# A mixture-of-experts stage that fetches its tokens row by row by indirect transfers in place of one-hot products

## The chip, the cores and the metric

One core of a Trainium2 chip runs the whole program. The metric is device time in microseconds (us), the median of several runs; smaller is better. The engines of the core are named as in the profile: PE (TensorE), DVE (VectorE), ACT (ScalarE), POOL (GpSimd), SP (SyncE, which here only issues transfers).

## The reference

Two layers of a hybrid network on 512 tokens of width 1024, all in fp32. Each layer mixes tokens (sparse attention, a gated delta rule, a convolution, an out-projection), normalizes, sends the tokens through a mixture of experts, and normalizes again. The change lies in the mixture of experts:

```python
g_w, g_idx = lax.top_k(softmax(xt @ w_group + b_group), 1)         # 1 of 4 groups
e_val, e_loc = lax.top_k(e_in, 2)                                  # 2 of its 8 experts
e_w = softmax(e_val) * g_w
...
hid = silu(xb @ w_gate[e]) * (xb @ w_up[e])                        # xb: the expert's tokens
y = hid @ w_down[e]                                                # 1024 -> 512 -> 1024
...
out[token] += y * e_w                                              # back to the token's row
```

There are 32 experts a layer, each with 6 MB of weights (gate, up, down), and 512 tokens times 2 experts = 1024 pairs.

## The kernel before, in words

**The MoE stage.** The router counts the tokens of each expert and sorts the experts by count. The sorted expert of rank r gets a fixed number of slots, `CAPS[r]` (L33): 192, 128, 96, 64 or 32. Nine *cycles* (`CYCLES`, L34) take the ranks in an order written out by hand; a cycle's experts fill up to 256 slots, in one or two *units* of 128. Cycle 0 holds two experts that are fixed beforehand (ranks 30 and 31, 64 slots each), so that work can begin before the sort is done; the other cycles hold two to five experts. There are 17 units a layer. Weights don't stay on the chip: each expert's come as six tiles of 1 MB, four of gate/up (`w_gu`, L1174, two transfers of 512 KB each) and two of down (`w_d`, L1179), all issued on SP in the order of the cycles, into a ring of 3 + 8 = 11 tiles (`ering`, L1162). A tile's transfer can start when the matmuls that read the tile's last content are done.

**What a cycle needs before its experts can run.** `prep_oh` (DVE, L1331 and L1339) compares the tokens' positions with a row of counts and so builds the one-hot matrix `m_oh` (512 tokens x up to 256 slots). `gather` multiplies it on PE with the normalized tokens (L1363). The tokens are kept as two rounded parts, `x1h` and `x1l` (split on ACT, POOL and DVE at L1193 and L1194 while the router works), so that fp32 values pass through the fast fp32r matmuls: 64 matmuls of 256 columns a cycle, in four pieces `kp`. `affine` (L1347 on ACT, L1349 on DVE) scales the result into `m_xe`, with the tokens' features on the partitions. `prep_ws` multiplies the one-hot with the router's weights (L1373) and picks each slot's weight (`m_wsl`, DVE L1380). `prep_T` transposes the one-hot on PE (L1388) and copies it (`m_ohT`, L232 on ACT or L234 on DVE) for the scatter.

**An expert.** `ffn` (L1251): gate/up matmuls `f_gu` (L1263 for 128 slots, L1267 for fewer), silu and weight on ACT and DVE (L1273, L1274), transposes `f_hT` (L1282) and their copy (L1284), down matmuls `f_y` (L1299). `y_split` (L1307, L1309) cuts the result into two fp32r parts, and `scatter` adds it to the tokens' rows: four matmuls `m_sc` with `m_ohT` (L1398) and an add on DVE (L1399) for each of 4 blocks of tokens.

**What sets the order.** PE runs this stage in program order. Inside `ffn`, while ACT and DVE make `f_h` and while `f_hTs` is copied, `fill` takes pieces from a queue (gather, prep_ws, prep_T, scatter) and so puts PE work there; the pieces of a cycle are spread over its experts, two places for each. The other engines are ordered by a scheduler that follows the program. A branch behind the nine cycles (L1468), for experts with more tokens than slots, isn't taken with these inputs. `residual` (behind the first expert) scales the tokens on POOL and loads the second normalization's weights on ACT's queue (L237).

## Time and profile before

| | us |
|---|---|
| median of 3 runs | 2047.71 (2028.74, 2047.71, 2047.86) |
| profiled execution, its own time | 2042.02 |
| its span, first to last instruction | 2040.3 |
| MoE stage of layer 0, first `f_gu` to last `f_y` | 448.5 to 995.5 |
| MoE stage of layer 1 | 1463.1 to 2009.4 |

The span is shorter than the time by 1.7 us, which lie around it. The mean granted PE clock of the profiled execution is 0.940 of 2.4 GHz. A timeline row gives start and length of a group of like instructions; lengths of neighbouring PE rows overlap, since matmuls are pipelined, so what a group costs on PE is read from the distance of the starts. Idle time stands in brackets with the event that ended it.

### The profile page before, as it was taken

How to read it: one execution, taken by the hardware profiler on the slowest of the kernel's cores; microseconds unless marked ns; L12 is line 12 of the kernel's file. 1: busy time of each engine (PE TensorE's matmuls, PEld its weight loads, DVE VectorE, ACT ScalarE, POOL GpSimd, SP SyncE). 2: the span in 40 equal slices, each digit the busy share in tenths (PEclk: the TensorE clock that was granted, in tenths of full speed). 3: DMA queues.
4: the chain of work that ended last, by engine and by line, in shares of the span. 5: the costliest groups of instructions: out<-in, count | busy, mean ns of one | idle time of the engine just before them, and what ended most of it. 6: DMA issues, size and time to landing. Idle time of an engine off the chain costs nothing. (4 is left out here: it accounts for less than half of the span.)

```text
span 2040.3 us, 33443 instructions
## 1 busy us (share of the span) xinstructions
PE 1858.5 (91%) x12956; PEld 1158.7 (57%) x12956; DVE 1028.8 (50%) x2148; ACT 600.3 (29%) x1275; POOL 363.3 (18%) x320
## 2 busy tenths in 40 slices
PE   8898799879999999998789988999699999999996
PEld 6776676654555545433378766767445555444433
DVE  2766866564332344323637777765543423443245
ACT  3333655432111111111233336453211111111122
POOL 2335632313000000000122356223130000000001
PEclk9997799989999999999989877989899999999998
DMA  5231001729999979888722310016299999798985
GB/s 174 90 96 63 1 12 35 272 81 351 403 408 386 357 281 408 311 304 325 272 94 83 104 42 1 23 61 252 88 354 404 408 372 350 293 408 311 334 318 193
DMA packets 141458, 465.41 MB, mean 228 GB/s; under 512 B 20345, under 2 KB 22897, under 8 KB 141297
## 3 DMA queue, kind: packets, MB, share of 16 engines
q1 hardware_dynamic: 137152, 452.54, 59.0%
q10 hardware_dynamic: 4144, 10.70, 1.5%
q8 instruction: 104, 1.70, 0.3%
q14 instruction: 58, 0.47, 0.1%
HBM read 459.00 MB, written 4.19 MB: 227 GB/s over the span
## 5 line engine op out<-in xcount | busy, mean ns | idle before, releaser
L1267 PE MATMUL f_gu<-w_gu,m_xe 128*32 128x256 f32 (+1 forms) x3456 | 391.9, 451 | 12.7 <-ACT m_xe L1347 6.2
L1267 PEld LDWEIGHTS f_gu<-w_gu,m_xe 128*32 128x32 f32 (+1 forms) x3456 | 134.0, 118 | 260.5 <-issue 200.4
L1299 PE MATMUL f_y<-w_d,f_hTs 128*32 128x256 f32 (+2 forms) x1824 | 250.1, 472 | 8.0 <-DVE m_wsl L1380 4.6
L1309 DVE TENSOR_TENSOR m_yl<-f_y,m_yh 32x256 fp32r<-32x256 f32 (+2 forms) x222 | 115.4, 520 | 260.6 <-ACT m_yh L1307 231.9
L1307 ACT CAST m_yh<-f_y 32x256 fp32r<-32x256 f32 (+2 forms) x222 | 98.3, 443 | 302.5 <-PE f_y L1299 300.3
L1274 DVE SCALAR_TENSOR_TENSOR f_h<-f_h,m_wsl,f_gu 128x128 f32<-128x128 f32 (+1 forms) x76 | 33.1, 435 | 292.3 <-ACT f_h L1273 291.8
L1299 PEld LDWEIGHTS f_y<-w_d,f_hTs 128*32 128x32 f32 (+2 forms) x1824 | 81.7, 123 | 152.6 <-issue 130.5
L1399 DVE TENSOR_TENSOR xr<-xr,m_sc 128x1024 f32<-128x1024 f32 x128 | 151.7, 1218 | 20.5 <-PE m_sc L1398 19.9
L1363 PE MATMUL m_g<-m_oh,x1h 128*128 128x256 f32 x576 | 146.7, 294 | 0.4 <-DVE m_oh L1339 0.3
L1363 PE MATMUL m_g<-m_oh,x1l 128*128 128x256 f32 x576 | 142.1, 286 | 0.0
L1273 ACT ACTIVATE f_h<-f_gu 128x128 f32<-128x128 f32 (+1 forms) x76 | 26.4, 347 | 350.0 <-PE f_gu L1267 258.0
L1398 PE MATMUL m_sc<-m_yh,m_ohT 128*128 128x512 f32 (+1 forms) x256 | 114.1, 446 | 14.8 <-DVE xr L1399 7.6
L1363 PEld LDWEIGHTS m_g<-m_oh,x1h 128*128 128x128 f32 x576 | 111.3, 193 | 15.6 <-issue 12.2
L344 POOL TENSOR_TENSOR w_hl<-w_slice,w_hl 128x512 fp32r<-128x512 f32 (+1 forms) x54 | 70.3, 1303 | 238.7 <-ACT w_hl L343 229.6
L216 POOL TENSOR_TENSOR ln_rs<-ln_rs,mhalf 128x1 f32<-128x1 f32 x16 | 8.6, 548 | 580.1 <-DVE ln_rs L293 580.1
L1363 PEld LDWEIGHTS m_g<-m_oh,x1l 128*128 128x128 f32 x576 | 111.5, 194 | 0.1
L1398 PE MATMUL m_sc<-m_yl,m_ohT 128*128 128x512 f32 (+1 forms) x256 | 102.1, 399 | 0.0
L343 ACT CAST w_hl<-w_slice 128x512 fp32r<-128x512 f32 (+1 forms) x96 | 56.0, 589 | 130.4 <-PE ipB L350 120.4
L879 POOL MEMSET vcb<- 128x512 f32 x2 | 1.0, 524 | 501.9 <-PE f_y L1299 501.7
L1263 PE MATMUL f_gu<-w_gu,m_xe 128*128 128x512 f32 x192 | 87.7, 603 | 0.0
L759 POOL TENSOR_TENSOR cvt<-cvt,cv_t 128x485 f32<-128x485 f32 (+28 forms) x66 | 78.3, 1187 | 13.8 <-ACT cv_t L755 12.0
L1398 PEld LDWEIGHTS m_sc<-m_yh,m_ohT 128*128 128x128 f32 (+1 forms) x256 | 48.8, 191 | 55.9 <-DVE xr L1399 22.2
(468 smaller groups left out, 3578.5 us busy)
## 6 DMA issues: line engine op xcount, KB each, us to landing
w_gu<-in_moe_w_gate SPq DMA_DIRECT2D x256, 512.0 KB, 10.9
w_gu<-in_moe_w_up SPq DMA_DIRECT2D x256, 512.0 KB, 10.4
w_d<-in_moe_w_down SPq DMA_DIRECT2D x128, 1024.0 KB, 11.4
w_slice<-in_w_in SPq DMA_DIRECT2D x20, 1024.0 KB, 5.2
w_out<-in_w_out SPq DMA_DIRECT2D x16, 1024.0 KB, 8.3
...
```

What stands on the lines that cost most here:

```text
L343: A.copy(hi[:, :n], src)
L344: (G if LOE(npc[0], k) else V).tensor_tensor(lo[:, :n], src, hi[:, :n].bitcast(F32), op=ALU.subtract)
L759: G.tensor_tensor(ac2[:, 30 - j:512], ac2[:, 30 - j:512], tm, op=ALU.add)
L1263: T.matmul(pg[:, i, :], xe(k), wv[:, i, :], start=(k == 0), stop=(k == 7), skip_group_check=True)
L1267: T.matmul(pg[j * c:(j + 1) * c, 0, 0:2 * fw], xe(k), wv[:, :, j * fw:(j + 1) * fw], start=(k == 0), stop=(k == 7), skip_group_check=True)
L1274: V.scalar_tensor_tensor(hh[:, :fw], hh[:, :fw], ws(), gu[:, fw:2 * fw], op0=ALU.mult, op1=ALU.mult)
L1299: T.matmul(o, lt, wv[:, n * nw:(n + 1) * nw], start=(k == 0), stop=(k == 3), skip_group_check=True)
L1307: A.copy(hi[:, n * nw:(n + 1) * nw], src[n])
L1309: V.tensor_tensor(lo[:, n * nw:(n + 1) * nw], src[n], hi[:, n * nw:(n + 1) * nw].bitcast(F32), op=ALU.subtract)
L1363: T.matmul(ps[:, kk * 256:kk * 256 + 256], src[t][:, k * P:(k + 1) * P], OH[cy][:, t, :], start=(t == 0 and i == 0), stop=(t == NT - 1 and ...
L1398: T.matmul(ps2[:, n, :], ohT[0:nr, t * P:(t + 1) * P], y[0:nr, n * 512:(n + 1) * 512], start=(i == 0), stop=(i == 1))
L1399: V.tensor_tensor(xr[t][:, :D], xr[t][:, :D], ps2.rearrange("p a b -> p (a b)"), op=ALU.add)
```

## The change

The one-hot products with the tokens are gone, and with them `x1h` and `x1l`. The normalized tokens are written to DRAM, block by block, on SP's queue (`x1D`). For each cycle a new step `index` multiplies the one-hot (now bf16) with a small matrix: each token's number in two bf16 parts, and the sorted weights in three bf16 parts, 98 columns in all. One such product of four matmuls a unit gives, for each slot, the token's number and the weights. DVE adds the parts, POOL issues an indirect transfer per unit (`tokens`), which fetches 128 rows of 4 KB from `x1D` into a tile `XG`; a slot without a token has a number above 511, and its row isn't fetched. `gather` is now eight PE transposes a unit out of `XG`, 16 a cycle. `prep_T` is one comparison on DVE of each slot's token number with a row of counts (`m_iot`), without PE. `index` of the next cycle goes to the front of the queue of `fill` when a cycle starts, and its gather stands in the queue behind the scatters that are left over. Cycle 0's tokens are fetched ahead of the loop, and its weights and `index(1)` come inside its first expert. The freed memory makes the ring 3 + 9 + 1 = 13 tiles. Lines after the change are shifted by 7 to 43.

The core of the diff:

```diff
-CN=32, XL="GGGV", ..., R=3, R2=8, NG=10, NE=15
+CN=32, ..., R=3, R2=9, R4=1, NG=10, NE=9
...
                 A.activation(xr[t][:, :D], xr[t][:, :D], AF.Identity, scale=rs, bias=nb)
+                nc.sync.dma_start(x1D[l][t * P:(t + 1) * P, :], xr[t][:, :D])
...
-            i = en[0] % (R + R2)
+            i = en[0] % (R + R2 + R4)
...
-            A.copy(av, xv)
-            (V if XL[t] == "V" else G).tensor_tensor(bv, xv, av.bitcast(F32), op=ALU.subtract)
...
+        XG = [x4(f"xg{i}") for i in range(2)]
+        for xg in XG:
+            G.memset(xg[:, :D], 0.0)
...
+        tw = small("r_tw", [P, NT, 98], BF16, bufs=1)
+        V.tensor_copy(tw[:, :, 0:2], tokb)
+        parts3(tw[:, :, 2:98], srt[:, :, 1, :], 32)
...
-            if width(cy) < 256:
-                V.tensor_scalar(ohv[:, :, width(cy):], ...)
...
+        def tokens(cy, ps, k):
+            tok, idx = small("m_tok", [P, 2]), small("m_idx", [P, 2], I32)
...
+                V.tensor_reduce(tok[0:n, u], v[0:n, u, 0:2], axis=AX.X, op=ALU.add)
+                V.tensor_scalar(idx[0:n, u], tok[0:n, u], float(PAD), None, op0=ALU.add)
+            for u in units(cy):
+                n = rows(cy, u)
+                G.indirect_dma_start(XG[u][0:n, :D], None, x1D[l][:, :], bass.IndirectOffsetOnAxis(ap=idx[0:n, u:u + 1], axis=0),
+                                     bounds_check=S - 1, oob_is_err=False)
...
+        def place_mm(cy, ps, k, rhs):
+            for u in units(cy):
+                for t in range(NT):
+                    T.matmul(ps[0:n, u * k:(u + 1) * k], OH[cy][:, t, u * P:u * P + n], rhs[:, t, :], ...)
...
+        def index(cy):
+            ps = bank("m_ix")
+            place_mm(cy, ps, 98, tw)
+            tokens(cy, ps, 98)
+            slot_weights(cy, ps, 98, 2, 32)
...
         def gather(cy, kp):
...
-                for t in range(NT):
-                    for i, src in enumerate((x1h, x1l)):
-                        T.matmul(ps[:, kk * 256:kk * 256 + 256], src[t][:, k * P:(k + 1) * P], OH[cy][:, t, :], ...)
+                for u in units(cy):
+                    m = rows(cy, u)
+                    T.transpose(ps[:, kk * 256 + u * P:kk * 256 + u * P + m], XG[u][0:m, k:1024:8], ident[0:m, 0:m])
...
         def prep_T(cy, u):
-            for t in range(NT):
-                T.transpose(ps[0:n, t * P:(t + 1) * P], OH[cy][:, t, u * P:u * P + n].bitcast(F32), ident)
-            evac(ohT[0:n], ps[0:n])
+            V.tensor_scalar(ohT[0:n], iot[0:n], TOK[cy][0:n, u:u + 1], None, op0=ALU.is_equal)
...
             if cy + 1 < len(JOBS):
                 prep_oh(cy + 1)
-                queue.extend([(gather, cy + 1, kp) for kp in range(4)] + [(prep_ws, cy + 1)])
+                if cy:
+                    queue.appendleft((index, cy + 1))
+                queue.extend((gather, cy + 1, kp) for kp in range(4))
```

**Where instructions move.** The start of layer 0's MoE stage on PE, before: the first gather is cut in two by the sort (`r_swp`, `r_sorted`, `r_ids`, `r_cnt`), and the first gate/up matmuls `f_gu` follow it.

```order
L1221 MATMUL r_swp<-ident,r_sw_3516 64x128 x2
L1363 MATMUL m_g_4189<-m_oh,x1h_4096 128x256
L1363 MATMUL m_g_4189<-m_oh,x1l_4097 128x256
...
L1226 MATMUL r_sorted<-r_pm,r_swT 128x64 x4
L1230 MATMUL r_ids<-r_pm,cst 1x32
L1238 MATMUL r_cnt<-r_pm,r_cntd 128x32
...
L1363 MATMUL m_g_4189<-m_oh,x1l_4109 128x256
L1267 MATMUL f_gu<-w_gu,m_xe_4187 64x512 x4
L1373 MATMUL m_ws<-r_sw_3516,m_oh 128x32 x4
```

After, the sort comes first; the product that places cycle 0's tokens (`m_ix`), four transposes out of the fetched rows (`xg`) and the first gate/up matmuls follow.

```order
L1223 MATMUL r_swp<-ident,r_sw_3520 64x128 x4
L1228 MATMUL r_sorted<-r_pm,r_swT 128x64 x4
L1245 MATMUL r_ids<-r_pm,cst 1x32
L1253 MATMUL r_cnt<-r_pm,r_cntd 128x32
L1382 LDWEIGHTS m_oh
L1382 MATMUL m_ix_4202<-tokb,m_oh 128x2
...
L1382 MATMUL m_ix_4202<-tokb,m_oh 128x2
L1417 MATMUL m_g_4214<-ident,xg_4107 128x128 x2
L1417 MATMUL m_g_4232<-ident,xg_4107 128x128 x2
L1282 MATMUL f_gu<-w_gu,m_xe_4200 64x512 x2
```

Between `m_ix` and `m_g` PE now waits for DVE's sums, POOL's transfer and its landing; 32 matmuls went out and 4 transposes came in.

In cycle 4 (ranks 20 and 0; `f_gu` of 32 slots is rank 20's), before: the fill places hold scatters (`m_sc`) of cycle 3 and the gather of cycle 5.

```order
L1267 MATMUL f_gu<-w_gu,m_xe_5509 32x256 x16
L1267 MATMUL f_gu<-w_gu,m_xe_5510 32x256 x16
L1398 MATMUL m_sc<-m_yh,m_ohT 128x512
L1398 MATMUL m_sc<-m_yl,m_ohT 128x512
...
L1398 MATMUL m_sc<-m_yl,m_ohT 128x512
L1282 MATMUL f_hT<-ident,f_h 128x128
L1398 MATMUL m_sc<-m_yh,m_ohT 128x512
...
L1398 MATMUL m_sc<-m_yl,m_ohT 128x512
L1363 MATMUL m_g<-m_oh,x1h_4096 128x256
L1363 MATMUL m_g<-m_oh,x1l_4097 128x256
```

After, `index(5)` stands ahead of the same scatters, and the transposes that need its rows behind them.

```order
L1282 MATMUL f_gu<-w_gu,m_xe_5351 32x256 x16
L1382 LDWEIGHTS m_oh
L1382 MATMUL m_ix<-r_tw,m_oh 128x98
...
L1382 MATMUL m_ix<-r_tw,m_oh 96x98
L1434 MATMUL m_sc<-m_yh,m_ohT 128x512
L1434 MATMUL m_sc<-m_yl,m_ohT 128x512
...
L1434 MATMUL m_sc<-m_yl,m_ohT 128x512
L1417 MATMUL m_g<-ident,xg_4107 128x128
L1417 MATMUL m_g<-ident,xg_4108 128x96
L1417 MATMUL m_g<-ident,xg_4107 128x128
```

Sixteen scatter matmuls and one `f_hT` lie between the last `m_ix` of cycle 5 and the first transpose of its rows.

DVE in the routing of layer 0, before: among the steps that pick the second expert (`r_em`, `r_m`, `r_s`, `r_mv`, `r_oh`) stand the last split of the tokens (`x1l`) and the clearing of the one-hot's unused columns (L1331).

```order
L1076 SCALAR_TENSOR_TENSOR r_em<-r_oh_4017,r_em 128x64
L1059 TENSOR_REDUCE r_m_4014<-r_em 128x2
L1061 SCALAR_TENSOR_TENSOR r_s_4016<-r_em,r_m_4014,cst 128x32 x2
L1194 TENSOR_TENSOR x1l_4109<-xr_3796,x1h_4108 128x1024
L1331 TENSOR_SCALAR m_oh<-cst 128x4x128
L1063 TENSOR_REDUCE r_mv<-r_s_4016 128x2
L1082 TENSOR_TENSOR r_m_4014<-r_m_4014,r_m_4013 128x2
L1064 TENSOR_TENSOR r_oh_4018<-r_s_4016,r_mv 128x64
```

After, the same steps follow each other directly.

```order
L1083 SCALAR_TENSOR_TENSOR r_em<-r_oh_4025,r_em 128x64
L1066 TENSOR_REDUCE r_m_4022<-r_em 128x2
L1068 SCALAR_TENSOR_TENSOR r_s_4024<-r_em,r_m_4022,cst 128x32 x2
L1070 TENSOR_REDUCE r_mv<-r_s_4024 128x2
L1089 TENSOR_TENSOR r_m_4022<-r_m_4022,r_m_4021 128x2
L1071 TENSOR_TENSOR r_oh_4026<-r_s_4024,r_mv 128x64
```

The two instructions between `r_s` and `r_mv` are gone here, and POOL no longer splits the tokens beside them.

## Rows read from the trace of the kernel before

**Rows 1.** The profile page: busy time of the engines (busy us, share of the span, instructions), and the span in 40 equal slices (GB/s moved by the DMA engines).

```profile
PE 1858.5 (91%) x12956; PEld 1158.7 (57%) x12956; DVE 1028.8 (50%) x2148; ACT 600.3 (29%) x1275; POOL 363.3 (18%) x320
...
GB/s 174 90 96 63 1 12 35 272 81 351 403 408 386 357 281 408 311 304 325 272 94 83 104 42 1 23 61 252 88 354 404 408 372 350 293 408 311 334 318 193
```

**Rows 2.** Windows of the span: the end of the routing in layer 0, the MoE stage of layer 0 (first gate/up matmul to last down matmul) and that of layer 1. Columns: window, its length, busy us of PE, PE weight loads, DVE, ACT and POOL with counts, granted clock, DMA share, GB/s.

```profile
426.60:432.40 5.80, 0.00 (x0) 0.00 (x0) 5.80 (x5) 3.84 (x2) 5.64 (x2) 0.50 0.00 0
...
448.50:995.50 547.00, 524.76 (x3789) 263.54 (x3787) 207.77 (x413) 99.38 (x231) 19.40 (x8) 0.98 0.92 352
...
1463.10:2009.40 546.30, 523.94 (x3788) 262.06 (x3787) 209.22 (x414) 99.11 (x230) 19.36 (x8) 0.99 0.92 351
```

**Rows 3.** What PE waited for in the MoE stage of layer 0, 448 to 995 us: total us, times, longest.

```profile
PE m_sc L1398 <- DVE m_ohT L234: 4.2, 4, 3.3
...
PE f_y L1299 <- DVE m_wsl L1380: 2.3, 1, 2.3
...
PE m_ohp L1388 <- DVE m_wsl L1380: 2.1, 2, 1.4
...
PE f_gu L1267 <- DMA w_gu<-in_moe_w_up: 1.0, 1, 1.0
```

**Rows 4.** What SP's DMA queue waited for in the same stage (total us, times, longest).

```profile
SPq L1174 <- PE f_y L1299: 94.9, 21, 15.1
SPq L1174 <- DMA w_d<-in_moe_w_down: 67.2, 35, 3.0
```

**Rows 5.** Windows of 40 us inside the MoE stage of layer 0, columns as in rows 2.

```profile
600.00:640.00 40.00, 39.09 (x157) 17.87 (x150) 15.74 (x22) 4.55 (x10) 0.00 (x0) 1.00 1.03 409
...
720.00:760.00 40.00, 39.57 (x230) 16.70 (x231) 17.47 (x27) 6.09 (x13) 0.00 (x0) 1.00 0.80 294
```

**Rows 6.** PE's timeline in layer 0 around the first expert's end and the gather of cycle 1. Columns: start us, length us, engine, line, operation, out<-in, tile shapes, count, and in brackets idle time before it with its releaser. The cut rows between 471.41 and 477.25 are 47 further gather matmuls, alternately from x1l and x1h; those between 477.25 and 479.72 are 16 more.

```profile
460.06 0.44 PE L1282 MATMUL f_hT<-ident,f_h 128*128 128x128 f32 x2 [1.00 <-DVE f_h L1274]
460.96 3.65 PE L1299 MATMUL f_y<-w_d,f_hTs 128*64 128x512 f32 x16 [0.46 <-ACT f_hTs L1284]
464.45 7.04 PE L1267 MATMUL f_gu<-w_gu,m_xe 128*64 128x512 f32 x32
471.41 0.39 PE L1363 MATMUL m_g<-m_oh,x1h 128*128 128x256 f32 x1
...
477.25 0.38 PE L1282 MATMUL f_hT<-ident,f_h 128*128 128x128 f32 x2
...
479.72 1.87 PE L1373 MATMUL m_ws<-r_srt,m_oh 128*128 128x32 f32 x16
481.42 0.63 PE L1388 MATMUL m_ohp<-ident,m_oh 128*128 128x128 f32 x4
481.98 3.65 PE L1299 MATMUL f_y<-w_d,f_hTs 128*64 128x512 f32 x16
```

**Rows 7.** PE's instructions in the MoE stage of layer 0, 448.5 to 995.5 us, grouped by line and form: count, busy us, mean ns of one, idle before.

```profile
L1363 PE MATMUL m_g<-m_oh,x1h 128*128 128x256 f32 x265 | 66.1, 290 | 0.1
L1363 PE MATMUL m_g<-m_oh,x1l 128*128 128x256 f32 x265 | 64.1, 282 | 0.0
```

**Rows 8.** Windows as in rows 2, of the scatter's matmuls (L1398) alone in the MoE stage of layer 0.

```profile
448.50:995.50 547.00, 74.69 (x256) 45.63 (x256) 0.98 0.92 352
```

**Rows 9.** PE's timeline where the out-projection's result is transposed with the column stride 8 that the change uses too (L1141).

```profile
389.87 1.16 PE L1141 MATMUL x1T_ps<-ident,xr 128*128 128x128 f32 x8 [2.20 <-DVE xr L1134]
390.79 0.48 PE L348 MATMUL opA<-wo_hi,mh 128*128 128x512 f32 x1
```

**Rows 10.** PE's timeline in the routing of layer 0 and at the start of its MoE stage; the rows left out are the first gather's, the sorting's and the counting's.

```profile
436.77 0.19 PE L1202 MATMUL r_pos<-r_selb,trib 128*128 128x32 bf16 x1 [13.13 <-DVE r_selb L1078]
...
436.91 0.27 PE L1204 MATMUL r_pos<-r_selb,oneb 128*128 128x32 bf16 x4
437.11 0.37 PE L1206 MATMUL r_pos<-oneb,r_selb 128*64 128x1 bf16 x4
...
448.56 0.65 PE L1267 MATMUL f_gu<-w_gu,m_xe 128*64 128x512 f32 x2
```

**Rows 11.** DVE's timeline in the routing of layer 0.

```profile
426.67 5.62 DVE L1061 SCALAR_TENSOR_TENSOR r_s<-r_em,r_m,cst 128x32 f32<-128x32 f32 x2
...
433.36 0.41 DVE L1061 SCALAR_TENSOR_TENSOR r_s<-r_em,r_m,cst 128x32 f32<-128x32 f32 x2
433.69 1.99 DVE L1194 TENSOR_TENSOR x1l<-xr,x1h 128x1024 fp32r<-128x1024 f32 x1
```

**Rows 12.** POOL's timeline in the same stretch.

```profile
426.58 5.66 POOL L1194 TENSOR_TENSOR x1l<-xr,x1h 128x1024 fp32r<-128x1024 f32 x2 [4.14 <-issue]
```

**Rows 13.** ACT and its DMA queue (ACTq) while the experts' weights stream: two 512 KB loads, and the instructions that wait for them.

```profile
464.67 0.33 ACTq L237 DMA_DIRECT2D ln_w<-in_ln_w  x1
465.04 0.87 ACTq L237 DMA_DIRECT2D ln_b<-in_ln_b  x1
...
473.33 1.06 ACT L1411 ACTIVATE ln_w<-ln_w 128x1024 f32<-128x1024 f32 x1 [7.49 <-DMA ln_w<-in_ln_w]
...
476.13 1.06 ACT L1412 ACTIVATE ln_b<-ln_b 128x1024 f32<-128x1024 f32 x1 [1.34 <-DMA ln_b<-in_ln_b]
```

**Rows 14.** SP's DMA queue: the first load that the MoE stage of layer 0 issues, and the last one.

```profile
450.54 0.39 SPq L1179 DMA_DIRECT2D w_d<-in_moe_w_down  x1
...
979.78 1.95 SPq L1179 DMA_DIRECT2D w_d<-in_moe_w_down  x2
```

More of the change, by code (lines that the diff above doesn't have):

```diff
@@ L173, in hybrid_kernel @@
     x_res = dr.tile([S, D], F32, name="x_res")
+    x1D = [dr.tile([S, D], F32, name=f"x1D{l}") for l in range(layers)]
     ident = cp.tile([P, P], F32, name="ident")
@@ L1349, in affine, with slot_weights @@
                 V.tensor_scalar(out_, in_, w1c[:, k:k + 1], b1c[:, k:k + 1], op0=ALU.mult, op1=ALU.add)
+        def tokens(cy, ps, k):
+            tok, idx = small("m_tok", [P, 2]), small("m_idx", [P, 2], I32)
+            v = ps[:, 0:2 * k].rearrange("p (u k) -> p u k", k=k)
+            full = all(rows(cy, u) == P for u in units(cy)) and len(units(cy)) == 2
+            for n, u in ([(P, slice(0, 2))] if full else [(rows(cy, u), slice(u, u + 1)) for u in units(cy)]):
+                V.tensor_reduce(tok[0:n, u], v[0:n, u, 0:2], axis=AX.X, op=ALU.add)
[4 more added lines that the diff above has]
+                                     bounds_check=S - 1, oob_is_err=False)
+            TOK[cy] = tok
+        def place_mm(cy, ps, k, rhs):
+            for u in units(cy):
+                n = rows(cy, u)
+                for t in range(NT):
+                    T.matmul(ps[0:n, u * k:(u + 1) * k], OH[cy][:, t, u * P:u * P + n], rhs[:, t, :], start=(t == 0),
+                             stop=(t == NT - 1), skip_group_check=True)
+        def slot_weights(cy, ps, k, o, m):
+            sums = small("m_wsum", [P, 2, 32])
+            for u in units(cy):
+                n = rows(cy, u)
+                V.tensor_reduce(sums[0:n, u, 0:m], ps[0:n, u * k + o:u * k + o + 3 * m].rearrange("p (a m) -> p m a", a=3),
+                                axis=AX.X, op=ALU.add)
+            w = small("m_wsl", [P, 8])
+            for i, (r, b, c, o_) in enumerate(JOBS[cy]):
+                s_, r = o_ % P, r if cy else r - 30
+                for j in range(P // c):
+                    V.tensor_copy(w[j * c:(j + 1) * c, i:i + 1], sums[s_:s_ + c, o_ // P, r:r + 1])
+            WS[cy] = w
+        def index(cy):
[3 more added lines that the diff above has]
+            slot_weights(cy, ps, 98, 2, 32)
         def gather(cy, kp):
@@ L1402, in hybrid_kernel @@
         prep_oh(0)
+        ps0 = bank("m_ix0")
+        place_mm(0, ps0, 2, tokb)
+        tokens(0, ps0, 2)
         for kp in range(GI):
@@ L1499, in hybrid_kernel @@
-                ox = t4("o_x")
-                psx = bank2("o_g")
-                for hh in range(2):
+                ow = small("o_w3", [P, NT, 3], BF16, bufs=1)
+                parts3(ow, wc.unsqueeze(2), 1)
+                pso = bank("o_ix")
+                for o, n, rhs in ((0, 2, tokb), (2, 3, ow)):
                     for t in range(NT):
-                        for i, src in enumerate((x1h, x1l)):
-                            T.matmul(psx[:, hh, :], oh[:, t * P:(t + 1) * P], src[t][:, hh * 512:(hh + 1) * 512],
-                                     start=(t == 0 and i == 0), stop=(t == NT - 1 and i == 1))
@@ L1506, in hybrid_kernel @@
-                A.copy(ox[:, 0:512], psx[:, 0, :])
-                V.tensor_copy(ox[:, 512:1024], psx[:, 1, :])
-                pso = bank2("o_ohp")
-                for t in range(NT):
-                    T.transpose(pso[:, 0, t * P:(t + 1) * P], oh[:, t * P:(t + 1) * P].bitcast(F32), ident)
-                for t in range(NT):
-                    T.matmul(pso[:, 1, 0:1], oh[:, t * P:(t + 1) * P].bitcast(F32), wc[:, t:t + 1], start=(t == 0),
-                             stop=(t == NT - 1))
@@ L1514, in hybrid_kernel @@
-                V.tensor_copy(oT, pso[:, 0, :])
-                ws = small("o_wsl", [P, 1], bufs=1)
-                V.tensor_copy(ws, pso[:, 1, 0:1])
+                        T.matmul(pso[:, o:o + n], oh[:, t * P:(t + 1) * P], rhs[:, t, :], start=(t == 0), stop=(t == NT - 1),
+                                 skip_group_check=True)
+                ot, oi = small("o_tok", [P, 1], bufs=1), small("o_idx", [P, 1], I32, bufs=1)
+                V.tensor_reduce(ot, pso[:, 0:2], axis=AX.X, op=ALU.add)
@@ L1567, in hybrid_kernel @@
         moe.close()
+        ring3.close()
         ring2.close()
```

78 lines of the change are left out of this document (40 added, 38 removed).

## The prediction

> **What bounds the kernel now.** The page comes first: PE is busy for 91% of the span, DVE for half [rows 1]. A share over the whole span hides stages, so the next view is the same line's GB/s: two plateaus of some eleven slices at 272 to 408, where the experts' weights stream [rows 1]. Windows around them give two MoE stages of 547.0 and 546.3 us, 1093 of 2040, with PE busy for 524.8 us of the first [rows 2]. In that stage PE waits only 1.0 us for weights and a few us for small DVE results [rows 3]; its own instruction stream sets the pace. SP's queue in turn waits mostly for PE: 94.9 us for down matmuls that still hold a ring tile, against 67.2 us for transfers of its own [rows 4]. In 40-us windows the stream alternates between 409 GB/s, which it does not exceed, and 294, where the ring holds it [rows 5]. So PE bounds the stage, with the stream close behind: 32 experts of 6 tiles of 1.0486 MB are 201.3 MB, 493 us at 408 GB/s. What PE loses is worth its full size only until the stream is the later one.
>
> **What goes from PE, per layer.** In the stage 265 + 265 gather matmuls run [rows 7]. From 471.41 to 477.25 there are 48, 0.122 us each [rows 6]: 530 x 0.122 = 64.5 us. The products for the weights take 1.70 us per 16 (479.72 to 481.42) and there are 136: 14.5. The one-hots' transposes take 0.56 us per 4 (481.42 to 481.98), 17 units: 9.5 [rows 6]. Together 88.5 us, all on the engine that sets the pace. Of the waits of DVE's copies behind those steps (4.2 + 2.3 + 2.1 us [rows 3]) I take 6 to go.
>
> **What comes to PE.** 17 units x 8 transposes, 4 of them ahead of the stage: 132. The transposes with the same stride take 0.92 us from start to next start for 8, with a length of 1.16 [rows 9]: 0.115 to 0.145 us each, 15 to 19 us; I take 16.5. The placement has 68 matmuls of bf16 with 98 columns. The trace has none like them: four bf16 matmuls of 32 columns lie within 0.20 us [rows 10], 0.05 each, and a gather matmul of 256 columns took 0.122; 3.4 to 8.3 us, and 6.8 (0.10 each), nearer to the wider one, since weight loads of 128 rows come with each. The fill places get emptier. Where nothing fills them, the first expert shows 1.00 us before `f_hT` and 0.46 before `f_y` [rows 6]; eight gathers now put 0.5 us per piece there, not 2, and some places are covered by scatters, so I take 5 us a layer, between 0 (all covered) and 10.
>
> **The new wait.** A gather's rows come through a chain: DVE's two small instructions (about 0.5 us, plus what stands ahead of them, 1.5 in all), two issues on POOL, and the landing. No transfer issued by POOL runs beside the weight stream before. The nearest rows are two loads of 512 KB on ACT's queue beside it: issued at 464.67 and 465.04, their waiters start at 473.33 and 476.13 [rows 13], so 8.7 and 11.1 us. A cycle's 256 rows are 1 MB, as these two together. I take D = 14 us from the last placement matmul to the last row landed; near the later load, with DVE and POOL ahead of it; bounds 5 (1 MB at 408 GB/s is 2.6 us, and the chain before it) and 30 (the 11.1 us nearly tripled, as single rows of 4 KB may be dearer than two plain loads). Against D stands what PE has to do between `m_ix` and the first transpose. By 4.7 us for 16 scatter matmuls (74.69 / 256 x 16 [rows 8]), 7.0 and 3.65 for the gate/up and down matmuls of a 64-slot expert [rows 6], half for 32 slots and twice for 128, the order gives for cycles 1 to 8 about 15, 26, 16, 19, 5, 26, 19 and 14 us. Only cycle 5 is short: 16 scatters and one `f_hT` lie between. PE is in program order, so behind the waiting transpose stand rank 20's down matmuls, which free ring tiles, and all of rank 0. At D = 14 this costs 9 us a layer, the other cycles nothing.
>
> The row shows 1 MB on one queue landing after 11.1 us while SP's queue streams [rows 13]. The Trainium skill (DMA: Bandwidth & Descriptors, Queues, rings and completion order) says that each DMA engine takes turns between the queues it has work for, packet by packet; with equal turns 1 MB would take about 5 us at half of 408 GB/s. The row stands between that and waiting behind the queued weights; by the rule D would be about 9 and cycle 5's wait 4 instead of 9 us, 10 us less over both layers.
>
> **PE's sum.** 547 - 88.5 - 6 + 16.5 + 6.8 + 5 + 9 = 490 us.
>
> **The stream's sum.** 13 tiles instead of 11 are ahead of the stage, so 179 follow: 187.7 MB, 460 us at 408 GB/s. The gathered rows are 1024 x 4 KB = 4.19 MB more, 10 us. The first load is issued 2 us after `f_gu` starts (448.56 [rows 10], 450.54 [rows 14]), and the last is issued 15.7 us ahead of the end (979.78 [rows 14], 995.5 [rows 2]), of which about 11 are its landing, as in rows 13, so some 4 are work behind it: 476 us as a floor. The two sums are now 14 us apart, and small experts use weights faster than they come, large ones slower; with a ring of 13 tiles (two experts) I add 3 us for it: 493, 54 us less than 547.
>
> **The head of the stage.** POOL's two splits of the tokens take 5.66 us from 426.58 [rows 12]; DVE's two small instructions beside them take 5.62, the same pair 0.41 at 433.36 [rows 11]. DVE's own split takes 1.99 more [rows 11], and PE waits 13.13 us for this chain [rows 10]. Without them the routing ends 5.2 + 2.0 + 0.4 = 7.6 us earlier. Of the path from 436.77 to 448.56 [rows 10], 11.8 us, the first gather, which the sort stood inside of, goes; in its place stand the placement, DVE's sums, and one unit's fetch without a stream beside it, 4 to 6 us, and four transposes and `affine`. I count that as 2.6 us longer, so a gain of 5 us a layer (-2 to +10). DVE's other new work (sums, three-part weights, comparisons of 512 columns in place of copies of 512) lies in a stage where it is busy 208 of 547 us [rows 2], and costs nothing unless it delays `m_idx`.
>
> The lock between POOL and DVE is in the trace: 2.8 us per instruction that otherwise takes 0.2 [rows 11, 12]. The Trainium skill (SBUF — State Buffer, SBUF: two separate sides) speaks against this change: a transfer issued on POOL needs descriptors which POOL writes, and it cannot while DVE holds the shared port. No run here shows it in that direction; a DVE pass over 128 x 1024 took 1.99 us [rows 11], and one such delay would make D 16: waits of 2 us more in cycle 5, 2 in cycle 8 and 1 in cycle 1, 10 us more over both layers.
>
> **Sum.** 2040.3 - 2 x (54 + 5) = 1922 of span, 1924 with the 1.7 us around it. The median of the runs is 1.0028 of the profiled execution (2047.71 / 2042.02): 1929 us.
>
> **The rivals.** *Slow fetches.* If D is large, every cycle waits, not only the fifth. By the list above the waits are 32 us at D = 20, 62 at 25, 100 at 30, where 9 are in my sum. The gain of 59 us a layer is used up at 59 + 9 = 68, D of about 26. At 30 the layer is 32 us longer than before: 2040.3 + 64, 2112 us as a median. For it: each fetch is 128 descriptors made by POOL, behind a saturated stream, and 14 is taken from plain loads. Against it: those plain loads were queued behind the same stream and took 11. At D = 20 the time is 1929 + 46 = 1975. *The stream decides, and fetches cost it more.* If the skipped rows of pads take their turns too, 17 x 128 rows are 8.9 MB, 22 us instead of 10, and the stream is held by the ring where experts are large: 505 us, 47 us gained a layer, 1953. For it: the 409 of rows 5 is a ceiling already reached; against: the change says that a pad's row is skipped. *More than forecast.* D of 5 to 8, no wait in cycle 5 (9 less) and placement at 0.05 (3 less): PE 478, the stream at 476; 74 us a layer, 1899. That the tokens aren't fetched per row, the change not doing what it says, has nothing for it: 132 transposes stand where 530 products stood.
>
> **How the numbers follow.** The forecast (D from 9 to 18) has 0.50, the stream with dearer fetches 0.17, more than forecast 0.15. Slow fetches have 0.18: 0.06 at D up to 24, still faster; 0.04 near 26, within 1%; 0.08 above. One per cent, 20 us, is about what a measurement of this kernel can tell from no change. Faster: 0.50 + 0.17 + 0.15 + 0.06 = 0.88; same 0.04; slower 0.08. The range goes from 1890, below the largest gain worked out, to 1995, D of nearly 22.
>
> **What would show it.** MoE stages of about 493 us from first `f_gu` to last `f_y`; PE waits for DMA `xg` of some 9 us once a layer, in rank 20's place in cycle 4; the rate near 400 GB/s over most of the stage; no DVE instruction of 2.8 us in the routing and PE's 13.13 us wait shorter by about 7. Waits for `xg` in most cycles, or a mean of 25 us from `m_idx` to `m_g`, would make me wrong; so would a stage of 493 with PE waiting for weights by tens of us, which would be the stream's bound, not PE's.

## The result and the profile after

The changed kernel takes 1965.74 us, the median of 4 runs (1956.32 to 1966.44), against 2042.12 for the kernel before in 4 runs; the ratio is 0.9624, with a 95% interval of 0.9563 to 0.9685. The forecast was 1929, the range 1890 to 1995. So the kernel is faster, as forecast, by about two thirds of the 118 us that were expected.

The page of the profiled execution, whose span is 1964.7 us: busy time, GB/s in the 40 slices, and POOL's own queue ([rows 1] of before):

```profile
PE 1743.3 (89%) x11812; PEld 1021.7 (52%) x11812; DVE 1009.4 (51%) x2258; ACT 573.8 (29%) x1250; POOL 387.3 (20%) x354
...
GB/s 179 87 86 76 12 12 12 264 152 284 408 402 405 403 323 383 409 374 409 249 110 82 90 64 2 12 43 267 138 320 409 402 403 405 305 399 408 362 409 181
...
q0 software_dynamic: 4736, 8.92, 1.3%
```

PE's busy time fell by 115 us, the span by 76. The plateaus of the two MoE stages are now at 402 to 409 GB/s for most of their length. POOL's queue moved 8.92 MB: 0.52 of it is `m_iot`, the rest 8.4 MB or 4.2 MB a layer, the rows of the 1024 token-expert pairs. A pad's row is not read; in the trace a packet of 4 bytes stands in its place.

The MoE stages of both layers (windows as in [rows 2]):

```profile
450.30:957.30 507.00, 467.81 (x3255) 198.95 (x3255) 206.39 (x447) 93.55 (x222) 36.77 (x25) 0.97 0.98 381
1424.70:1934.00 509.30, 471.64 (x3255) 199.40 (x3255) 205.00 (x447) 93.52 (x223) 36.26 (x24) 0.96 0.97 380
```

Two windows of 40 us inside the first stage, as in [rows 5]:

```profile
570.00:610.00 40.00, 31.60 (x281) 15.43 (x281) 14.30 (x23) 7.60 (x19) 0.00 (x0) 1.00 1.03 407
...
690.00:730.00 40.00, 39.32 (x142) 13.83 (x141) 5.24 (x10) 5.79 (x11) 0.00 (x0) 1.00 0.82 305
```

From 570 to 610 the stream runs at its 407 GB/s and PE is busy for 31.6 of 40 us; from 690 to 730, in the expert of 192 slots, PE is full and the stream is held. In the kernel before, PE was busy for 39.1 of 40 us beside a stream of 409 GB/s [rows 5].

What PE waited for in that stage, beside [rows 3]:

```profile
PE m_sc L1434 <- DVE xr L1435: 14.3, 12, 3.6
PE f_gu L1282 <- DMA w_gu<-in_moe_w_up: 10.0, 10, 1.6
PE f_hT L1297 <- DVE f_h L1289: 5.0, 5, 2.3
PE m_g L1417 <- DMA xg<-x1D,m_idx: 1.7, 2, 0.9
...
PE f_y L1314 <- ACT f_hTs L1299: 1.5, 3, 0.6
```

The wait for weights went from 1.0 to 10.0 us, and a wait that had been small, of the scatter's matmuls for the add on `xr`, is now the largest, 14.3 us. The wait for fetched rows, for which the sum had 9 us, is 1.7. SP's queue, beside [rows 4]:

```profile
SPq L1184 <- DMA w_d<-in_moe_w_down: 99.9, 50, 3.7
...
SPq L1189 <- PE f_y L1314: 42.8, 12, 10.2
...
SPq L1184 <- PE f_y L1314: 18.3, 13, 5.2
```

Its waits for down matmuls (94.9 us at L1174 before, and 18.5 at L1179) are 18.3 at the first of these lines, now L1184, and 42.8 at the second, now L1189; those for transfers of its own `w_d` rose from 67.2 to 99.9.

Where the 75.6 us of span came from, by the first profile of each kernel (times from the trace):

| stretch | forecast | measured |
|---|---|---|
| start to the first matmul `opA` of layer 0's out-projection (361.1, 371.0) | 0 | +9.9 |
| `opA` to the first `f_gu`, layer 0 (87.5, 79.3) and 1 (87.9, 80.2) | -5, -5 | -8.2, -7.7 |
| MoE stage, layer 0 (546.9, 507.0) and 1 (546.2, 509.2) | -54, -54 | -39.9, -37.0 |
| end of layer 0's stage to `opA` of layer 1 (379.8, 387.2) | 0 | +7.4 |
| end of layer 1's stage to the end (31.0, 30.9) | 0 | -0.1 |

Of the 42 us by which the forecast had too much, 31 lie in the stages and 17 outside them; the heads gave 6 more than was counted.

### The profile page after: what moved, and what is told of

The parts are those of the page before. It is cut to its first block, busy times and chain, and to the rows that moved or that the text cites. A ratio compares the mean times of both kernels' runs of the same rounds, so it can differ in the third digit from the quotient of the medians.

```text
span 1964.7 us, 31355 instructions
## 1 busy us (share of the span) xinstructions
PE 1743.3 (89%) x11812; PEld 1021.7 (52%) x11812; DVE 1009.4 (51%) x2258; ACT 573.8 (29%) x1250; POOL 387.3 (20%) x354
## 3 DMA queue, kind: packets, MB, share of 16 engines
q0 software_dynamic: 4736, 8.92, 1.3%
## 5 line engine op out<-in xcount | busy, mean ns | idle before, releaser
L1282 PE MATMUL f_gu<-w_gu,m_xe 128*32 128x256 f32 (+1 forms) x3456 | 398.6, 454 | 19.9 <-DMA w_gu<-in_moe_w_up 17.8
L1314 PE MATMUL f_y<-w_d,f_hTs 128*32 128x256 f32 (+2 forms) x1824 | 258.1, 480 | 9.9 <-ACT f_hTs L1299 2.9
L1374 POOL DMA_INDIRECT xg<-x1D,m_idx x34 | 35.9, 1056 | 744.3 <-PE f_hT L1297 331.2
L1435 DVE TENSOR_TENSOR xr<-xr,m_sc 128x1024 f32<-128x1024 f32 x128 | 152.8, 1218 | 25.5 <-PE m_sc L1434 24.6
L1288 ACT ACTIVATE f_h<-f_gu 128x128 f32<-128x128 f32 (+1 forms) x76 | 26.4, 348 | 383.1 <-PE f_gu L1282 289.5
L1020 ACT ACTIVATE e<-a_s,a_nm 128x128 f32<-128x128 f32 (+3 forms) x128 | 66.5, 526 | 45.9 <-DVE a_nm L1015 38.7
L1417 PE MATMUL m_g<-ident,xg 128*128 128x128 f32 (+2 forms) x272 | 47.8, 299 | 19.4 <-DMA xg<-x1D,m_idx 16.1
L351 DVE TENSOR_TENSOR w_hl<-w_slice,w_hl 128x512 fp32r<-128x512 f32 (+1 forms) x42 | 30.0, 715 | 64.3 <-ACT w_hl L350 64.1
L1278 PEld LDWEIGHTS f_gu<-w_gu,m_xe 128*128 128x128 f32 x192 | 35.0, 191 | 53.2 <-issue 48.9
L1015 DVE TENSOR_REDUCE a_nm<-a_s 128x1 f32<-128x384 f32 (+3 forms) x88 | 55.0, 634 | 11.0 <-PE a_s L1012 10.2
## 6 DMA issues: line engine op xcount, KB each, us to landing
w_gu<-in_moe_w_gate SPq DMA_DIRECT2D x256, 512.0 KB, 12.1
w_d<-in_moe_w_down SPq DMA_DIRECT2D x128, 1024.0 KB, 12.1
```

The costliest lines, as they stand in the source:

```text
L351: (G if LOE(npc[0], k) else V).tensor_tensor(lo[:, :n], src, hi[:, :n].bitcast(F32), op=ALU.subtract)
L1015: V.tensor_reduce(nm[:, 0:hb], ps[:, :hb * L].rearrange("p (h l) -> p h l", h=hb), axis=AX.X, op=ALU.max, negate=True)
L1020: A.activation(e[:, :L], ps[:, i * L:(i + 1) * L], AF.Exp, bias=nm[:, i:i + 1], accum_out=sums[:, i0 + i:i0 + i + 1])
L1278: T.matmul(pg[:, i, :], xe(k), wv[:, i, :], start=(k == 0), stop=(k == 7), skip_group_check=True)
L1282: T.matmul(pg[j * c:(j + 1) * c, 0, 0:2 * fw], xe(k), wv[:, :, j * fw:(j + 1) * fw], start=(k == 0), stop=(k == 7), skip_group_check=True)
L1314: T.matmul(o, lt, wv[:, n * nw:(n + 1) * nw], start=(k == 0), stop=(k == 3), skip_group_check=True)
```

## The experiments

Two theories stood against each other on the stage. A: PE sets the pace, and what is missing is cover that was lost, above all on DVE. B: the weight stream is as late as PE, and what PE gains turns into waits for weights. All experiments compare the MoE stage of layer 0, whose instructions on PE are in the same order in all variants of the changed kernel, but for those that one variant leaves out; the change's stage is 507.0 us there, 508.4 in its second profile. In layer 1 the same two profiles have 509.2 and 505.4, so 2 to 4 us in one run are no finding.

**The burst on DVE.** The first look is at the changed kernel's longest such stall, in cycle 4. DVE's timeline behind `index(5)`:

```profile
668.39 0.21 DVE L1370 TENSOR_REDUCE m_tok<-m_ix 128x1 f32<-128x2 f32 x2
...
668.85 0.41 DVE L1352 TENSOR_TENSOR m_oh<-cst,r_srt 128x256 bf16<-128x256 f32 x1
...
669.59 0.20 DVE L1371 TENSOR_SCALAR m_idx<-m_tok 128x1 int32<-128x1 f32 x2
...
670.04 2.51 DVE L1396 COPY m_wsl<-m_wsum 64x1 f32<-64x1 f32 x16
672.59 2.35 DVE L1435 TENSOR_TENSOR xr<-xr,m_sc 128x1024 f32<-128x1024 f32 x2
```

PE's in the same place:

```profile
662.36 1.93 PE L1314 MATMUL f_y<-w_d,f_hTs 128*32 128x256 f32 x32
...
667.68 0.54 PE L1382 MATMUL m_ix<-r_tw,m_oh 128*128 128x98 bf16 x8
...
673.86 0.80 PE L1434 MATMUL m_sc<-m_yh,m_ohT 96*128 96x512 f32 x1 [3.61 <-DVE xr L1435]
...
678.48 0.48 PE L1417 MATMUL m_g<-ident,xg 128*128 128x128 f32 x1 [0.84 <-DMA xg<-x1D,m_idx]
679.84 0.80 PE L1417 MATMUL m_g<-ident,xg 96*128 96x96 f32 x3 [0.88 <-DMA xg<-x1D,m_idx]
680.57 3.64 PE L1314 MATMUL f_y<-w_d,f_hTs 128*32 128x256 f32 x32
```

The scatter's adds (L1435) free its PSUM tiles. They stand behind sums, one-hot compares and 16 copies of weights (L1396, 2.51 us), and the next scatter waits 3.61 us. In three windows, of the wait, of the 10 us behind it and of what follows:

```profile
670.30:673.80 3.50, 0.00 (x0) 0.00 (x0) 3.28 (x17) 0.27 (x1) 1.97 (x2) 1.00 1.02 403
673.80:684.20 10.40, 8.62 (x45) 4.57 (x45) 4.97 (x9) 0.54 (x1) 0.00 (x0) 0.51 1.03 386
684.20:700.00 15.80, 15.80 (x45) 4.99 (x44) 1.69 (x4) 1.45 (x4) 0.00 (x0) 1.00 1.02 402
```

PE is idle for 3.5 us, and then runs for 10 us at a granted clock of 0.51, the lower of its two levels: the down matmuls that start at 680.57 take 3.64 us, where 32 of the same shape took 1.93 at 662.36. So such a wait costs more than its own length. The first experiment takes the copies off DVE:

```diff
-                    V.tensor_copy(w[j * c:(j + 1) * c, i:i + 1], ...)
+                    (A.copy if cy else V.tensor_copy)(w[j * c:(j + 1) * c, i:i + 1], ...)
```

> The changed kernel, with the 14 to 16 small copies of slot weights (m_wsl) of cycles 1 to 8 on ACT instead of DVE; PE's order is the same. Theory A (cover lost): behind each index DVE has a burst of small work, 2.5 us of it these copies, and the adds that free the scatter's PSUM tiles wait behind it, so PE's waits of m_sc for xr, 14.3 us a layer in the changed kernel, fall to 6 or less, the MoE stage of layer 0 goes from 507 to about 498 us, and the time falls by 12 to 18 us. Theory B (stream): the weight stream holds the stage, so what PE gains is waited for w_gu; the waits for weights rise from 11 us by as much as the others fall, and the stage stays at 505 or more.

Measured: 1954.47 us (ratio 0.9566, 0.9498 to 0.9634), 11 below the changed kernel where A had 12 to 18; stages 503.9 and 503.8, between A's 498 and the changed kernel's. Its waits in layer 0:

```profile
PE f_gu L1282 <- DMA w_gu<-in_moe_w_up: 12.1, 14, 1.5
PE m_sc L1434 <- DVE xr L1435: 6.0, 10, 1.5
PE f_y L1314 <- ACT f_hTs L1299: 4.8, 6, 1.3
PE m_g L1417 <- DMA xg<-x1D,m_idx: 3.9, 2, 3.2
```

A's mechanism holds: the scatter's wait fell from 14.3 to 6.0. But only 3 to 4.5 us of the 8.3 stayed: weights took 2 to 3 (10.0, in the second profile 9.1, to 12.1), ACT's burst 3.3 (`f_hTs`, 1.5 to 4.8), the fetch 2.2; `f_hT`'s wait for `f_h` on DVE fell by 2.4. Both theories have a part.

**The ring.**

```diff
-R2=9, R4=1
+R2=8, R4=0
```

> The changed kernel with the ring of 11 weight tiles of before (8 instead of 9 in the second part, none in the third). Theory B (stream): two tiles less ahead of the stage are 2.1 MB more to load inside it, 5 us at 408 GB/s, and the ring holds the stream more often while large experts run; MoE stage of layer 0 longer by 8 to 15 us, waits for weights above 18 us. Theory A (PE sets the pace, weights are a side matter): stage longer by less than 4 us, waits for weights within 3 us of 11.

Measured: 1992.88 us, the median of three of its runs (a fourth took 4335.45 us, which nothing on record explains); ratio 0.9747, 0.9668 to 0.9827; stages 521.3 and 520.5:

```profile
PE f_gu L1282 <- DMA w_gu<-in_moe_w_up: 17.4, 18, 1.6
```

The scatter's wait is 14.3 again, the weights' is 17.4, the stage 13 to 14 us longer: B. Of the 40 us that the stage gained, these two tiles are 14. The kernel before with one tile less is the counterpart:

```diff
-R2=8
+R2=7
```

> The kernel before with a ring of 10 tiles instead of 11. First question, what a tile is worth where PE sets the pace: theory A0 (PE bounds the stage of before) expects the MoE stage of layer 0 within 3 us of 547, theory B0 (the stream mattered as much there) 552 or more; in the changed kernel two tiles less cost 14 us. Second question, the mixer of layer 1, from the end of layer 0's stage to the first opA, 380 and 383 us in the kernel before and 384 to 396 in eight runs of the changed body: any edit makes the scheduler rearrange that mixer (363 of 1858 PE instructions here, 603 to 971 with the change). Theory F (the rearranged order and the clock make it vary): 384 to 396 here too. Theory G (the change itself lengthens it): 379 to 384.

Its stage of layer 0 is 548.9 us, 2 longer, as A0 expects; layer 1's is 553.7, 7.5 to 11 longer than in the two profiles of before (546.2 and 542.8), so a tile was not free there either. PE's wait for weights in layer 0:

```profile
PE f_gu L1267 <- DMA w_gu<-in_moe_w_up: 3.4, 3, 1.6
```

**The stream's bytes, PE's pace alone, the stream's pace alone.** The next three leave out work in layer 0, which also sends other tokens to layer 1's experts; only layer 0 is compared. Each is a single run.

```diff
-                G.indirect_dma_start(XG[u][0:n, :D], ...)
+                if cy < 2:
+                    G.indirect_dma_start(XG[u][0:n, :D], ...)
```

> The changed kernel without the fetches of cycles 2 to 8 (their tiles keep older rows; that part of the computation is wrong). It measures what the fetches cost: the wait for them, and their bytes in the stream. Theory A (PE sets the pace): only the waits for xg go, 1.7 us, stage of layer 0 at 503 to 508 us. Theory B (the stream holds the stage as much as PE): 3.5 MB less, 9 us of stream, so the stage is shorter by 5 to 10 and waits for weights fall from 10 to 6 or less.

Measured: stage 498.4, 9 to 10 us shorter. Its wait for weights:

```profile
PE f_gu L1282 <- DMA w_gu<-in_moe_w_up: 3.0, 4, 1.6
```

The waits for rows were 1.7 to 2.0 us, so 7 to 8 us remain for the bytes, and the wait for weights is 6 to 7 shorter. 3.5 MB at 408 GB/s are 8.6 us: B, at nearly its full size.

```diff
+                ne[0] += 1
+                if r not in weights and ne[0] % 4 == 0:
+                    weights[r] = last[0]
```

> The changed kernel, in which every fourth expert uses the weights of the expert before it and loads none (144 instead of 192 tiles a layer). It measures PE's pace without the stream. Theory A (PE sets the pace): waits for weights, 10 to 11 us, go, and the stage of layer 0 stands at 495 to 499. Theory B (the stream's waits also cost clock and knock-on waits): the stage falls below 492.

Measured: stage 493.2, no wait for weights. Window of the stage:

```profile
441.80:935.00 493.20, 465.67 (x3255) 198.44 (x3255) 206.11 (x447) 93.53 (x222) 36.21 (x24) 0.97 0.78 290
```

This is between the two expectations: the 11 us of waits and about 3 more. It is PE's own pace in the changed kernel, all DVE waits included.

```diff
         def scatter(cy, u, t):
+            if 1 < cy < 8:
+                return
```

> The changed kernel without the scatters of cycles 2 to 7 (their results are left out of the output): some 190 matmuls, 56 us of PE a layer, and their waits, are gone. It measures the stream's pace without much of PE. Theory B (the stream is within a few per cent of PE): the stage of layer 0 falls only to 480 to 492 us, with waits for weights above 40 us. Theory A (PE sets the pace by a margin): it falls by the whole 56 to 70 us towards 440 to 450, which the sum of the stream (476 us) denies.

Measured: stage 496.9, 10 us shorter. Its window:

```profile
449.90:946.80 496.90, 429.99 (x3063) 167.99 (x3063) 152.04 (x399) 93.35 (x222) 36.10 (x25) 0.94 0.99 389
```

Its waits:

```profile
PE f_gu L1282 <- DMA w_gu<-in_moe_w_up: 22.2, 23, 1.6
PE f_hT L1297 <- DVE f_h L1289: 12.6, 14, 2.3
```

The scatter's own line shrank by 57 us (76.3 to 19.6 of busy time), PE's busy time by 38 (467.8 to 430.0, at a granted clock of 0.94 in place of 0.97), the stage by 10. The other 28 are new idle time: 12 more for weights (10.0 to 22.2), 9.5 more for rows of which one wait of 9.6 holds nearly all, because the scatters that covered that fetch are gone, 13 more for small results (`f_hT` for `f_h`, 5.0 to 12.6; `f_y` for `f_hTs`, 1.5 to 6.9) and 5 in small pieces, less 12 that the scatters had waited themselves. The waits for weights above 40 that B expected didn't come, so this run does not single out the stream, and the stream's pace without PE, which it was meant to show, stays a sum. What it shows is that PE's own work no longer sets the length: three quarters of what was taken off PE here came back as waiting.

**Toward a better version.** One tile more, paid with a working tile, an `m_ohT` buffer and an `m_wsum` buffer, and the copies on ACT:

```diff
-R2=9, R4=1, NG=10, NE=9
+R2=9, R4=2, NG=10, NE=8
```

> The changed kernel with the copies of slot weights on ACT, and a ring of 14 tiles, for which one working tile, one m_ohT buffer and one m_wsum buffer are given up. Two tiles less cost 14 us a layer, so theory B expects 4 to 7 us a layer from one more: stage of layer 0 at 497 to 500, time 10 us below that of the copies on ACT alone. Theory A (PE's own waits are what is left): no gain, or a loss by waits for the buffers given up (m_xe, m_yh, m_ohT).

Measured: 1947.59 us (0.9543, 0.9483 to 0.9602), stages 497.2 and 494.8: 7 to 9 us a layer below those with the copies on ACT alone, at the top of what B expected or above it, and no wait for the buffers given up. The time is 7 us below that of the copies alone, not 10: the first fetch now holds PE for 9.93 us, where the changed kernel has 6.47:

```profile
445.44 1.12 PE L1417 MATMUL m_g<-ident,xg 128*128 128x128 f32 x4 [9.93 <-DMA xg<-x1D,m_idx]
```

With those copies on POOL:

> The ring of 14 tiles with the copies of slot weights on POOL instead of ACT. With them on ACT, f_y waited 4.8 us a layer for f_hTs, which ACT copies too (1.5 in the changed kernel). Theory A (ACT's burst is what the copies now cost): waits of f_y for f_hTs back to 2, m_sc for xr still 6, stage of layer 0 at 494 to 496 instead of 497.2. Theory B (what PE gains there is waited for weights): stage within 1 us of 497.2.

Measured: 1945.98 us (0.9538, 0.9477 to 0.9599), stage 497.7. `f_y` waits 1.5 us for `f_hTs` again, but POOL does the copies in front of the fetch:

```profile
661.97 4.47 POOL L1396 COPY m_wsl<-m_wsum 64x1 f32<-64x1 f32 x16 [29.86 <-DVE m_wsum L1390]
666.71 1.04 POOL L1374 DMA_INDIRECT xg<-x1D,m_idx  x1 [0.27 <-POOL m_wsl L1396]
```

and PE's wait for rows in the stage is 10.4 us instead of 4.1. The gain on ACT was lost on POOL's queue; the stage stays at that of the first ring of 14, as B expected, but not by B's cause alone.

The row numbers computed straight from PSUM, so that `m_idx` comes first on DVE:

```diff
-V.tensor_reduce(tok[0:n, u], v[0:n, u, 0:2], axis=AX.X, op=ALU.add)
-V.tensor_scalar(idx[0:n, u], tok[0:n, u], float(PAD), None, op0=ALU.add)
+for uu in range(u.start, u.stop):
+    V.tensor_scalar(idx[0:n, uu:uu + 1], v[0:n, uu, 0:1], v[0:n, uu, 1:2], float(PAD), op0=ALU.add, op1=ALU.add)
+V.tensor_reduce(tok[0:n, u], v[0:n, u, 0:2], axis=AX.X, op=ALU.add)
```

> As the ring of 14 tiles with POOL's copies, and DVE computes the row numbers in one instruction straight from PSUM, which puts m_idx ahead of the one-hot compares of cycle 1 (1.5 us earlier in the head). In the ring of 14 the head's wait for xg was 9.9 us, in the changed kernel 6.5. Theory E (the first fetch queues behind the dynamic weights that are issued at that moment, 1 MB with 13 tiles, 2 MB with 14): issued ahead of most of them it lands 3 us or more earlier than by the 1.5 us alone; wait for xg in the head 5 to 6 us, first f_gu 13 us behind r_pos instead of 17. Rival (the landing takes its time whatever is queued): wait 8.4, head 15.5.

The kernel that ran has the copies on ACT, not on POOL as the text says, so it stands beside the first ring of 14. Measured: 1943.42 us (0.9532, 0.9474 to 0.9589), stage 495.5, and 15.4 us from `r_pos` to `f_gu` instead of 17.2. PE's wait for the first fetch:

```profile
444.10 1.12 PE L1418 MATMUL m_g<-ident,xg 128*128 128x128 f32 x4 [8.16 <-DMA xg<-x1D,m_idx]
```

That is the rival's figure: PE's wait lost 1.8 us, little more than the 1.5 by which the fetch was issued earlier, though it now went out 0.2 us ahead of the weights. The same edit alone, in the changed kernel:

> The changed kernel with the row numbers in one instruction alone. Theory E: head 11 to 12 us instead of 13.3 (1.5 us earlier, and ahead of 1 MB of weights). In the stage every fetch starts about 0.5 us earlier, which changes nothing, since the waits for xg there are 1.7 us: stage within 2 us of 507, time 2 to 6 us below that of the changed kernel.

Measured: 1942.72 us (0.9512, 0.9452 to 0.9571), the best of all, level with the ring of 14. Both expectations failed. The head is 13.4 us, as before the edit. And the stages are 499.1 and 496.4, 8 to 13 us shorter. What moved is DVE's order, which the scheduler made anew (PE's is the same in the stage). Behind `index(6)`, before the edit:

```profile
732.56 1.58 DVE L1396 COPY m_wsl<-m_wsum 32x1 f32<-32x1 f32 x10
734.17 2.35 DVE L1435 TENSOR_TENSOR xr<-xr,m_sc 128x1024 f32<-128x1024 f32 x2
```

```profile
735.45 0.79 PE L1434 MATMUL m_sc<-m_yh,m_ohT 128*128 128x512 f32 x1 [3.45 <-DVE xr L1435]
```

With it:

```profile
727.41 1.21 DVE L1436 TENSOR_TENSOR xr<-xr,m_sc 128x1024 f32<-128x1024 f32 x1
728.55 2.22 DVE L1397 COPY m_wsl<-m_wsum 64x1 f32<-64x1 f32 x14
```

```profile
728.68 0.50 PE L1435 MATMUL m_sc<-m_yh,m_ohT 128*128 128x512 f32 x1 [1.23 <-DVE xr L1436]
```

One add on `xr` now stands ahead of the small copies, where two stood behind them. The waits for the adds in the stage, 14.3 us before:

```profile
PE m_sc L1435 <- DVE xr L1436: 9.4, 12, 2.5
```

The wait for the add is 5 us less in all: 2.2 here, and 2.4 in the cycle after next, where a wait of 2.39 is gone. Behind `index(5)`, shown above, it is not shorter (1.63 and 2.51 for 3.61); there only the lower clock behind it lasts 6.8 us for 10.2. In all, idle time of PE is 4 us less, and PE is busy for 463.7 us instead of 467.8 and 468.6, at a granted clock of 0.98 over the stage for 0.97 in both profiles of the changed kernel: together 8 to 9. Set side by side instruction by instruction, the two runs part at these three places by 4, 4 and 2 us and come 2 us nearer elsewhere. Theory A has its full size here. That the order did it, and not the fetches' earlier issue, rests on these places: the wait for rows fell by 1.4 to 1.7 us only.

**The stretches outside.** Both kernels once more:

> The changed kernel once more, for a second profile. In the first one its layer 0 reached the routing's end 9 us later than the kernel before did up to the out-projection, with nearly the same order of instructions and a lower granted clock. Theory C (the clock differs from execution to execution): the start of the out-projection in layer 0 (first opA) moves by several us from 371.0. Theory D (the change delays the mixer): it stands within 1 us of 371.0 again.

> The kernel before once more, for a second profile. Theory C (the clock differs from execution to execution): the first opA of layer 0 moves by several us from 361.1. Theory D (the order or the loads of the changed kernel delay its mixer): it stands within 1 us of 361.1, 9 to 10 us ahead of the changed kernel's.

The changed kernel ran 1961.44 us (span 1959.7) with the first `opA` at 362.6, not 371.0; in nine of its variants, whose orders on PE there are the same, it stands between 362.1 and 372.0. The kernel before has it at 361.4 again. So 8.4 us of the +9.9 in layer 0 are a difference between two executions of one program (theory C). They differ in the granted clock there (from 200 to 260 us 0.61 in the first, 0.76 in the second). Whether the change makes the late arrival more frequent stays open: five of the eleven profiles with its body are at 367.6 or later, none of the three with the body of before (361.1, 361.4, 362.6).

The stretch ahead of layer 1's `opA` is another matter: 379.8, 383.1 and (ring of 10) 382.8 us with the body of before, 384.4 to 396.9 in eleven runs with the change's. Here too one program moves by 8 us (387.2 and 395.5 in the two profiles of the changed kernel), but in PE's busy time, 333.2 and 342.2. Its idle time is 48.6 to 54.2 us in all eleven and 40.6 to 44.5 in the three of before. So the change's body has some 10 us more idle time there, in a part whose text it does not touch but whose order on PE the scheduler made anew. The ring of 10, which moved fewer instructions, added at most 4 us of it, which speaks for theory G; which moves cost the time stays open.

## Why the prediction was right or wrong

**Faster, by PE's removed work.** Right. PE's busy time in the stage fell from 524.8 to 467.8 us; the sum had 459.6 (524.8 - 88.5 + 16.5 + 6.8). The placement was 4.8 for 6.8, the transposes 22.8 for 16.5:

```profile
450.30:957.30 507.00, 22.77 (x132) 18.09 (x132) 0.97 0.98 381
...
450.30:957.30 507.00, 4.79 (x68) 3.72 (x68) 0.97 0.98 381
```

0.17 us a transpose, not 0.125: the row that I read had eight in one run; here 14 of the 23 runs have four or two, which took 0.15 to 0.54 us each, and the longer runs mostly 0.13 to 0.16. The same work also took longer, at a granted clock of 0.97 for 0.98: the scatter has the same 256 matmuls as in [rows 8] and takes 76.3 for 74.7 us, and all of `f_gu`, `f_y` and the scatter took 7.7 us more. Against that, the three groups that went were busy for 93.7 us by their own lines, 5 more than the 88.5 of the sum. The 5 us for fill places without cover came as 4.5 (waits of `f_hT` for `f_h` and of `f_y` for `f_hTs`, 2.0 us before, 6.5 after).

```profile
450.30:957.30 507.00, 76.31 (x256) 45.90 (x256) 0.97 0.98 381
```

**The new wait, 9 us in cycle 5.** Wrong in size, right in place. POOL's issues and the transposes (above) show D: the last placement matmul ends at about 668.2, the rows of both units are there at 679.84, 11.6 us, where I took 14; the two waits are 0.84 and 0.88 us. That D came near is partly luck: I took it for 256 rows, 1 MB, and in this cycle POOL's queue moved 0.34 MB. The slack was larger than the 5 us that I counted, because the scatters in it waited 3.6 us for DVE and then ran at the lower clock, so that DVE's delay stood where I expected the wait for the rows. The issues:

```profile
670.47 1.01 POOL L1374 DMA_INDIRECT xg<-x1D,m_idx  x1 [40.67 <-PE f_hT L1297]
671.79 0.96 POOL L1374 DMA_INDIRECT xg<-x1D,m_idx  x1 [0.30 <-issue]
```

**DVE's new work costs nothing.** This step failed. I named DVE's share, 208 of 547 us, as its cover, and a delay of `m_idx` as the one way to a cost. What mattered was where the work stands: a burst of 4 us behind each index, in front of the adds which free the scatter's tiles. Before, those waits were small:

```profile
PE m_sc L1398 <- DVE xr L1399: 2.8, 10, 0.6
```

Cost: 11.5 us of waits in the stage (14.3 for 2.8), plus the time at the lower clock behind them; the row numbers straight from PSUM, alone in the changed kernel, got 8 to 9 back by a new order on DVE.

**3 us for the interplay of PE and stream.** The mis-sized term. PE alone is 493.2 us (with three quarters of the weights), where my sum had 490; both together are 507.0. So the interplay costs 14 us. That 490 lies so near 493.2 is partly luck: the sum has 7 us too much for the rows and nothing for the adds' 11.5. Two resources 14 us apart in their sums (476 and 490) aren't hidden behind each other: experts of 32 slots wait for weights (rows above, 31.6 of 40 us), the one of 192 slots holds the stream (305 GB/s), and a ring of two experts evens out only a part. That also shows in each single step: 14 us for two tiles, 9 to 10 for 8.6 us of bytes, 10 for 57 us of scatter.

**The head, 5 us a layer.** Right, and somewhat small: 8.2 and 7.7 from `opA` to `f_gu`. In layer 0 the routing ends 10.2 us earlier (I had 7.6), and the path behind it is 2.0 us longer (I had 2.6). The lock between POOL and DVE is gone (the pair of 5.62 us takes 0.41), PE's wait of 13.13 us [rows 10] is 5.10, and for the rows PE waits 6.47 us, of which the fetch itself, from issue to landing, is 4.3. I had written of a fetch without a stream beside it; the thirteenth tile's weights, 1 MB, were on their way with it:

```profile
436.50 0.19 PE L1204 MATMUL r_pos<-r_selb,trib 128*128 128x32 bf16 x1 [5.10 <-DVE r_selb L1085]
...
449.11 1.11 PE L1417 MATMUL m_g<-ident,xg 128*128 128x128 f32 x4 [6.47 <-DMA xg<-x1D,m_idx]
```

**Nothing elsewhere.** Wrong by 14 to 17 us, whichever profiles of the two kernels are compared: 9.9 ahead of layer 0's `opA` and 7.4 ahead of layer 1's in the first pair, 1.2 and 12.4 in the second. The prediction counted nothing outside the stages and their heads; the idle time in layer 1's mixer, which the scheduler rearranged, is the part that every run shows.

**The rivals.** Slow fetches did not come: about 8 us from issue to landing on the page. The stream's bound came, though without the pads' bytes of that rival, and 1953 was nearer than the forecast. The range's upper end, 1995, had been drawn for a D of 22. That the result lies within the range is in part luck: fetches did not fill it, but terms that the sum had too small or not at all.
